# A hybrid decoder trunk on one core: a PSUM bank lent to the recurrences, and values turned by one VectorE transpose with ScalarE copies

## The chip, the cores and the metric

The kernel runs on one core of one Trainium2 chip. The metric is the device time of one execution in microseconds (us). The engines that matter are TensorE (PE in the profile: matmuls; PEld: its weight loads), VectorE (DVE), ScalarE (ACT) and SyncE (SP), which issues the DMAs. PSUM, where matmuls accumulate, is used as eight banks of 128 partitions x 512 f32.

## The reference

One layer of a decoder trunk, for 256 tokens of one new sequence and 8 x 8 tokens of running sequences: 320 columns of tokens, named TOK, in every large matmul. Two token mixers run side by side on one joint projection of x, an mLSTM matrix memory (4 heads) and an HGRN2 linear recurrence (8 heads).

```python
proj = jnp.einsum('btd,de->bte', x, w_in)          # q, k, v, gates of both mixers
h, C, n, m = _mlstm(q, k, v, ig, lf, C0, n0, m0)    # 4 heads, dk 256, dv 512
branch_a = norm(h) * ml_norm_g * sigmoid(ml_o)
o, S = _hgrn2(hq, log f, 1 - f, hg_i, S0)           # 8 heads, dk 128, dv 256
branch_b = rms(o) * hg_norm_g * silu(hg_g)
merged = sigmoid(gate_a) * (branch_a @ w_a) + sigmoid(gate_b) * (branch_b @ w_b)
x1 = LayerNorm(alpha * x + merged @ w_out)
y  = LayerNorm(alpha * x1 + relu(x1 @ w_up)^2 @ w_down)
```

## The kernel before

**Main work.** All projections are cut into 304 tiles of 128 output channels x 320 tokens. A tile has one PSUM bank (a *main* bank, `take` at L545) and 48 matmuls: 16 pieces of the inner dimension, each as three products of split f32 values, `xh` with `wh`, `xl` with `wh` and `xh` with `wl` (high and low halves). A tile's weights come as two *units* of 128x1024, of 24 matmuls each. `prep` (L478) readies a unit: ScalarE rounds the raw weights to the high half (`wh<-wr`), VectorE subtracts to get the low half (`wl<-wr,wh`, L497). There are three buffers for this, so the copy of unit u can start when TensorE has finished unit u−3.

**Side work.** Between the main matmuls stand the small matmuls, copies and transposes of the two recurrences. Each takes a bank from a pool of *side* banks, `sbank`; before the change main has banks 0 to 2 and side banks 3 to 7 (L338, L339). The tiles come in the order of the projection's kinds: q and k of the mLSTM heads, its values (`mv`), then HGRN heads with three kinds of tiles each, with the mLSTM's output gate (`o`) behind them and the HGRN gate (`hg`) behind that.

**What sets the order.** The program is straight-line code, and a scheduler in Python (`Sched`, L144) writes it: each piece of side work is a generator (a chain) that yields an engine, a cost in ns and the instruction. `act` (L261), `dve` (L265) and `dve_t` (L269) give the costs of ScalarE copies, VectorE operations and VectorE transposes. The scheduler adds the costs up to clocks of its own, and issues a chain's next instruction when its clocks say that operands are ready. So the costs decide the order on each engine, and the chip then runs each engine's instructions in that order, with real waits. All ScalarE instructions go through the helper at L350, all plain matmuls through L356.

**The turn.** Values leave their tile as x: channels on partitions, tokens on columns (128 x n x 320, n = 4 blocks for an mLSTM head, 2 for an HGRN head). The recurrences need tokens on partitions. `turn` (L1145) does it in 24 VectorE transposes: for each of 4 groups of 32 partitions, four for the prompt's tokens (L1156, 32 x 64n elements) and two for the others (L1159, 32 x 32n), each of which transposes its 32x32 blocks and puts them on the partitions where they belong. It is called by `m_V` (L948) and by `h_i` (L1474).

**Behind the turn in `h_i`.** ScalarE copies the high half of the turned sample tokens to `rh` (64x256), VectorE subtracts for the low half (L1488, L1492 in the changed kernel), and then two *spread* matmuls `rh,ra` of 128x256 (L356) read `rh`. `h_out` (L1604) computes an HGRN head's outputs, normalises two blocks of 128x256 (`rms`, a ScalarE copy of a bank with an accumulator read), transposes them on VectorE (L1631) and stores them. `ev_o` (L1691) multiplies the mLSTM's normalised output by its gate and splits it to high and low halves for the branch's projection.

Of the kernel before, what the change touches and what calls it, by code (L numbers as in the profile page):

```python
# [20 lines left out]
TOK = 320  # L21
KT = 16
MH, DK, DV = 4, 256, 512
HH, HK, HV = 8, 128, 256
# [220 lines left out]
def wait(*evs):  # L245
    return ("wait", evs)


def acq(pool, n=1):
    return ("acq", pool, n)  # L250


def rel(pool, item):
    return ("rel", pool, item)


def post(ev):
    return ("set", ev)


def act(n, psum=False, ptr=0):  # L261
    return ((61 if psum else 112) + n) / 1.2 + 93 * ptr


def dve(n, psum=False, mode=1, ptr=0):  # L265
    return ((62 if psum else 66) + n / mode) / 0.96 + 55 * ptr


def dve_t(n):  # L269
    return 155.0 + 1.07 * n  # L270


def pe_f(n, m=128):
    return max(212.0 if m == 128 else 162.0, n * 1.66)
# [20 lines left out]
def by_row(ap, off, gap):  # L295

    return cap(ap, off, [[32, 4], [8, 2], [1, 8]] if gap else [[8, 4], [32, 2], [1, 8]])
# [16 lines left out]
class Program:  # L314
# [48 lines left out]
    def carve(self):  # L363
# [12 lines left out]
        self.Part = Part  # L376
        A, B, C, R = Part(self.f1), Part(self.f2), Part(self.f3), Part(self.ra[:, 0:6400])

# [5 lines left out]
        self.vr = Pool([A.three(4, 320)])  # L384
        self.kw = Pool([B.three(2, 320)])
        self.bc = Pool([B(712) for _ in range(2)])
        self.eb0 = B(512)
        self.eb = Pool([self.eb0])
        self.stg = Pool([B(256) for _ in range(2)])
        self.qn0 = B(256)  # L390
        self.qn = Pool([self.qn0])
# [190 lines left out]
    def before(self, i, t):  # L582
        s = self.s
        kind, h, c = t[:3]
        if kind == "mv" and c == 0:
            s.until(lambda: self.vr.free and self.qk.free)
            self.m_start(h)
            self.vr.free.sort(key=lambda x: x[0])
            self.mh[h]["vr"] = self.vr.free.pop(0)[1]
        elif kind == "hf":  # L590
            s.until(lambda: self.hs.free)
            if h == 0:
                s.spawn(self.m_after(), 0)
            self.h_start(h)
        elif kind == "o" and h == 0:
            s.until(lambda: all(m["end"].t is not None for m in self.mh))
        elif kind == "hg" and h == 0:
            s.until(lambda: all(m["end"].t is not None for m in self.hh))
            self.carve_m()
            self.carve_b()  # L600
            B = self.Part(self.f2)
            for pool in (self.sg, self.sg, self.sr, self.ld, self.ld, self.ld):
                pool.free.append((s.t["pe"], B(320)))
        if kind in ("o", "wa", "hg", "wb"):
            s.spawn(self.fetch(kind, h), 1)
        elif kind == "mk" and h == 0 and c == 0:
            self.load_ev.t = s.t["pe"]
            self.dma(self.lmask, self.d["lmask"])
        elif kind == "wo" and h == 0:
            s.until(lambda: len(self.sbank.free) >= 5)  # L610
            self.mbank.free += self.sbank.free[:3]
            del self.sbank.free[:3]
            self.hl_free += [(s.t["pe"], x) for x in self.wx[:4]]
            R = self.Part(self.wxv[4].rearrange("p x s v -> p (x s v)"))
            self.lns = [R.three(2, TOK) for _ in range(3)]
            s.spawn(self.ln_x(), 1)
        elif kind == "dn" and c == 3 and h == 0:
            self.carve_x()
        elif kind == "dn" and c == 0 and h == 0:
            s.spawn(self.xs_(), 0)  # L620
        elif i == len(TILES) - 8:
            for j in range(MH):
                s.spawn(self.m_C(j), 3)
            for j in range(HH):
                s.spawn(self.h_S(j), 3)
# [363 lines left out]
    def m_KW(self, h):  # L989
# [13 lines left out]
        m["khl"] = khl  # L1003
        kh, kl = khl[:, 0], khl[:, 1]
        yield ("dve", dve_t(512), lambda: v.transpose(kw[:, :, 0:256], kw[:, :, 0:256]))
        yield ("act", act(512), lambda: self.A(kh.rearrange("p s k -> p (s k)").rearrange("p (c t) -> p c t", c=2), kw[:, :, 0:256]))
        yield ("dve", dve(512), lambda: v.tensor_tensor(kl, kw[:, :, 0:256], kh.bitcast(F32), ALU.subtract))
# [137 lines left out]
    def turn(self, to, x):  # L1145

        v = self.nc.vector
        n = x.shape[1]
        for a in range(4):
            p = slice(32 * a, 32 * a + 32)  # L1150
            col = lambda y: y.rearrange("p (c a k) -> p a c k", a=4, k=32)[:, a]
            for b in range(4):
                q = slice(32 * b, 32 * b + 32)
                i = x[p, :, 0:NP_].rearrange("p c (i b k) -> p b i c k", b=4, k=32)[:, b]
                o = to[q, 0:2, :].rearrange("p i (c a k) -> p a i c k", a=4, k=32)[:, a]
                yield ("dve", dve_t(64 * n), lambda: v.transpose(o, i))  # L1156
            for b in range(2):
                o, i = col(to[64 + 32 * b:96 + 32 * b, 2, :]), x[p, :, NP_ + 32 * b:NP_ + 32 * b + 32]
                yield ("dve", dve_t(32 * n), lambda: v.transpose(o, i))  # L1159

    def later(self):
        e = Ev()
# [452 lines left out]
    def h_out(self, h):  # L1615
        nc, v, m = self.nc, self.nc.vector, self.hh[h]
        if h:
            yield wait(self.hh[h - 1]["o"])
        yield wait(m["aT"], m["I"])
        at, it = m["at"], m["it"]  # L1620
        on = yield acq(self.on)
        yield post(m["o"])
        b = yield acq(self.sbank)
        yield ("pe", pe_f(256), lambda: self.mm(b[:, 0:256], at[:, 0:128], it[:, 0, :], start=True, stop=True))
        yield ("pe", pe_f(256), lambda: self.mm(b[:, 256:512], at[:, 368:496], it[:, 0, :], start=True, stop=False))
        yield ("pe", pe_f(256), lambda: self.mm(b[:, 256:512], at[:, 128:256], it[:, 1, :], start=False, stop=True))
        for i in range(2):
            yield from self.rms(b[:, 256 * i:256 * i + 256], on[:, i, :], 128)
        yield rel(self.sbank, b)
        for i in range(2):  # L1630
            yield ("dve", dve_t(256), lambda: v.transpose(on[:, i, :], on[:, i, :]))  # L1631
        yield from self.place(self.rows_to(self.oH[h]), on[:, 0:2, :].rearrange("p i v -> p (i v)").rearrange("p (b c) -> p b c", c=32))
        done = self.later()
        yield wait(m["S"])
        ob = m["ob2"]
        yield from self.rms(ob[:, 0:256], on[:, 2, :], 128)
        yield rel(self.sbank, ob)
        yield rel(self.at, at)
        b = yield acq(self.sbank)
        for j in range(2):  # L1640
            yield ("pe", PE_T, lambda: nc.tensor.transpose(b[:, 128 * j:128 * j + 128], on[:, 2, 128 * j:128 * j + 128], self.ident))
        o = yield acq(self.ho)
        for j in range(2):
            yield ("act", act(64, True), lambda: self.A(by_row(o, 64 * j, False), by_row(b, 128 * j, True)))
        yield rel(self.sbank, b)
        yield ("sp", 620, lambda: self.dma(
            self.oL[h].rearrange("(j p) t -> p j t", p=128), o[:, 0:128].rearrange("p (j t) -> p j t", t=64)))
        for j in range(2):
            yield post(self.oT_ev[2 * h + j])
        yield wait(self.later())  # L1650
        yield rel(self.ho, o)
        yield wait(done)
        yield rel(self.on, on)
        yield wait(m["SP"], m["sdone"])
        yield rel(self.it, it)
        yield rel(self.hs, m["set"])
        yield post(m["end"])
# [33 lines left out]
    def ev_o(self, j, c, b):  # L1691
        v = self.nc.vector
        g = yield acq(self.sg)
        r = yield acq(self.sr)
        yield from self.sigmoid(b[:, :TOK], g, r, ((self.mbank, b),))
        yield rel(self.sr, r)
        x = yield from self.fetched("o", j)
        yield ("dve", dve(TOK, ptr=1), lambda: v.scalar_tensor_tensor(g, g, self.vec[:, V_MLG + j:V_MLG + j + 1], x, ALU.mult, ALU.mult))  # L1698
        yield rel(self.ld, x)
        yield from self.split(g, self.bah[:, j, :], self.bal[:, j, :])  # L1700
        yield rel(self.sg, g)
        yield post(self.ba_ev[j])
# [386 lines left out]
```

## Time and profile before

| | us |
|---|---|
| median of 3 runs | 2304.08 |
| lowest, highest | 2303.45, 2305.43 |
| the profiled execution: its time | 2302.73 |
| the profiled execution: its span | 2300.8 |
| busy: PE, DVE, ACT | 2289.6, 1458.9, 1036.6 |

The granted TensorE clock was 0.999 on the mean. The span is the stretch from the first to the last instruction that the profiler recorded. A row of a timeline is: start in us from the span's start, length in us, engine, line, operation, what is written, `<-`, what is read, shapes, count; in brackets the idle time before it and what ended it. A row of groups has the count, then the busy time in us and the mean of one in ns. A row of waits has engine, operand and line, what it waited for, and the total in us, the number of times and the longest. Names: `f`, `f3h` and `f3m` are scratch, `it` and `iv` of the code among them; `bank` is any PSUM bank; `rh` and `ra` are operands of side matmuls.

### The profile page before, as it was taken

The page shows a single profiled execution, that of the slowest core. Times are in us where ns is not written, and L with a number is a line of the kernel's source. Part 1 is how long each engine was busy: PE and PEld are TensorE (multiplying, and loading weights), DVE is VectorE, ACT ScalarE, POOL GpSimd, SP SyncE. Part 2 cuts the span into 40 slices and gives each one's busy share as a digit, 9 for nine tenths or more (in the row PEclk, how much of TensorE's full clock was granted, in tenths as well). Part 3 has the DMA queues.
Part 4 walks back from the last instruction along what each step waited for, and adds up shares of the span by engine and source line. Part 5 has one row for each costly group of instructions (what it writes and reads, how often), then busy time and mean ns, then how long its engine had stood idle before and what let it go on. Part 6 is the DMA issues. An engine that isn't in the chain of part 4 may idle for free.

```text
span 2300.8 us, 38921 instructions
## 1 busy us (share of the span) xinstructions
PE 2289.6 (100%) x15592; PEld 2246.1 (98%) x15592; DVE 1458.9 (63%) x2634; ACT 1036.6 (45%) x1653; POOL 13.5 (1%) x37
## 2 busy tenths in 40 slices
PE   9999999999999999999999999999999999999998
PEld 9999899999999999999999999999999999999998
DVE  6786786788888886555555767654444444444455
ACT  5443445455555565444433446533433343234334
POOL 0000000000000000000000000000000000000000
PEclk9999999999999999999999999999999999999999
DMA  7667977755565564555545644444444444444475
GB/s 284 211 186 259 295 250 229 259 176 185 191 207 187 166 198 167 180 174 170 176 172 175 214 163 147 147 147 149 154 147 150 152 147 153 149 147 154 149 228 193
DMA packets 214574, 424.94 MB, mean 185 GB/s; under 512 B 83572, under 2 KB 110068, under 8 KB 213368
## 3 DMA queue, kind: packets, MB, share of 16 engines
q1 hardware_dynamic: 209512, 415.97, 53.7%
q0 software_dynamic: 4736, 6.29, 1.0%
q8 instruction: 122, 2.00, 0.3%
q14 instruction: 60, 0.49, 0.1%
q10 hardware_dynamic: 144, 0.20, 0.0%
HBM read 371.48 MB, written 50.90 MB: 184 GB/s over the span
## 4 chain that ended last, share of the span: by engine, by line
PE 69%; DVE 3%; ACT 1%; issue 0%; ACTq 0%; DVEq 0%
PE bank L356 69%; DVE wl L497 1%; ACT wh L350 0%; DVE f L1156 0%; DVE f L1445 0%; ACT f L350 0%; DVE f3m L1973 0%; DVE f3m L1980 0%; ACT f3m L350 0%; DVE f L1159 0%; DVE f L1315 0%; DVE f L1316 0%; DVE f L1631 0%; DVE f L1698 0%; DVE f L1309 0%
## 5 line engine op out<-in xcount | busy, mean ns | idle before, releaser
L356 PE MATMUL bank<-xh,wh 128*128 128x320 f32 (+1 forms) x2504 | 794.6, 318 | 0.0
L356 PE MATMUL bank<-xh,wl 128*128 128x320 f32 (+1 forms) x2504 | 774.8, 310 | 0.0
L356 PE MATMUL bank<-xl,wh 128*128 128x320 f32 (+1 forms) x2504 | 772.2, 309 | 0.0
L497 DVE TENSOR_TENSOR wl<-wr,wh 128x1024 fp32r<-128x1024 f32 x440 | 538.7, 1224 | 361.4 <-ACT wh L350 358.3
L350 ACT ACTIVATE wh<-wr 128x1024 fp32r<-128x1024 f32 x440 | 465.4, 1058 | 524.7 <-PE bank L356 495.6
L356 PEld LDWEIGHTS bank<-xh,wh 128*128 128x128 f32 x2504 | 472.0, 189 | 17.2 <-issue 15.3
L356 PEld LDWEIGHTS bank<-xl,wh 128*128 128x128 f32 x2504 | 471.5, 188 | 3.3
L356 PEld LDWEIGHTS bank<-xh,wl 128*128 128x128 f32 x2504 | 471.8, 189 | 0.2 <-DVE wl L497 0.2
L497 DVE TENSOR_TENSOR bb<-wr,bb 128x1024 fp32r<-128x1024 f32 x162 | 198.5, 1225 | 193.7 <-ACT bb L350 193.5
L350 ACT ACTIVATE bb<-wr 128x1024 fp32r<-128x1024 f32 x162 | 171.6, 1059 | 294.6 <-PE bank L356 277.5
L356 PE MATMUL bank<-ra,wh 128*128 128x320 f32 x1008 | 275.9, 309 | 0.7 <-DVE ra L1672 0.7
L356 PE MATMUL bank<-ra,bb 128*128 128x320 f32 x1096 | 255.2, 309 | 0.0
L356 PE MATMUL bank<-xh,bb 128*128 128x320 f32 (+1 forms) x1136 | 253.8, 309 | 0.0
L356 PE MATMUL bank<-rxb,bb 128*128 128x320 f32 x1088 | 249.0, 309 | 0.0
L356 PEld LDWEIGHTS bank<-xh,bb 128*128 128x128 f32 x1136 | 191.0, 188 | 0.0
L356 PE MATMUL bank<-rxb,wh 128*128 128x320 f32 x608 | 187.5, 308 | 0.0
L356 PE MATMUL bank<-rxb,wl 128*128 128x320 f32 x608 | 187.5, 308 | 0.0
L356 PEld LDWEIGHTS bank<-ra,bb 128*128 128x128 f32 x1096 | 184.9, 187 | 0.0
L356 PEld LDWEIGHTS bank<-rxb,bb 128*128 128x128 f32 x1088 | 184.2, 187 | 0.0
L356 PEld LDWEIGHTS bank<-ra,wh 128*128 128x128 f32 x1008 | 180.9, 187 | 0.9 <-DVE ra L1672 0.9
L356 PE MATMUL bank<-xl,bb 128*128 128x320 f32 (+1 forms) x568 | 175.5, 309 | 0.0
L356 PE MATMUL bank<-bb,wh 128*128 128x320 f32 (+1 forms) x536 | 119.0, 313 | 0.0
(259 smaller groups left out, 2244.4 us busy)
## 6 DMA issues: line engine op xcount, KB each, us to landing
wr<-wt SPq DMA_DIRECT2D x602, 512.0 KB, 3.3
rx<-C SPq DMA_DIRECT2D x34, 256.0 KB, 5.6
Cs<-rx SPq DMA_DIRECT2D x34, 256.0 KB, 4.8
f<-C SPq DMA_DIRECT2D x30, 256.0 KB, 5.5
Cs<-f SPq DMA_DIRECT2D x30, 256.0 KB, 4.1
f<-first SPq DMA_DIRECT2D x6, 704.0 KB, 9.6
vD<-ra SPq DMA_DIRECT2D x4, 1024.0 KB, 5.2
f<-S SPq DMA_DIRECT2D x8, 512.0 KB, 5.0
```

What stands on the lines that cost most here:

```text
L350: return self.nc.scalar.activation(out, in_, func, **kw)
L356: self.nc.tensor.matmul(*a, **kw)
L497: self.V().tensor_tensor(lo, raw, hi.bitcast(F32), ALU.subtract)
```

## The change

Five edits:

1. *Banks.* At the first `mk` tile (keys of the first mLSTM head) one main bank is moved to the side pool; at the first `hg` tile, when both recurrences have ended, it is given back. In between main work has two banks and side work six.
2. *The turn.* One VectorE transpose of the whole x in place (128x1280 for an mLSTM head, 128x640 for an HGRN head; L1152) does all 32x32 blocks; the 24 pieces are then copied to their places by ScalarE (`self.A`), each planned as ready when the transpose ends.
3. *The cost of a transpose* in the planner goes from 155 + 1.07n to 295 + 1.05n ns.
4. `h_out` transposes its two blocks in one operation of 128x512 instead of two of 128x256.
5. `ev_o` waits, from block 7 on, until the last HGRN head has reached "aT" or "sdone" before it splits.

```diff
--- before.py
+++ after.py
@@ -267,7 +267,7 @@
 
 
 def dve_t(n):
-    return 155.0 + 1.07 * n
+    return 295.0 + 1.05 * n
 
 
 def pe_f(n, m=128):
@@ -598,12 +598,15 @@
             s.until(lambda: all(m["end"].t is not None for m in self.hh))
             self.carve_m()
             self.carve_b()
+            self.mbank.free.append(self.sbank.free.pop())
             B = self.Part(self.f2)
             for pool in (self.sg, self.sg, self.sr, self.ld, self.ld, self.ld):
                 pool.free.append((s.t["pe"], B(320)))
         if kind in ("o", "wa", "hg", "wb"):
             s.spawn(self.fetch(kind, h), 1)
         elif kind == "mk" and h == 0 and c == 0:
+            s.until(lambda: self.mbank.free)
+            self.sbank.free.append(self.mbank.free.pop())
             self.load_ev.t = s.t["pe"]
             self.dma(self.lmask, self.d["lmask"])
         elif kind == "wo" and h == 0:
@@ -1146,6 +1149,7 @@
 
         v = self.nc.vector
         n = x.shape[1]
+        t = yield ("dve", dve_t(TOK * n), lambda: v.transpose(x, x))
         for a in range(4):
             p = slice(32 * a, 32 * a + 32)
             col = lambda y: y.rearrange("p (c a k) -> p a c k", a=4, k=32)[:, a]
@@ -1153,10 +1157,10 @@
                 q = slice(32 * b, 32 * b + 32)
                 i = x[p, :, 0:NP_].rearrange("p c (i b k) -> p b i c k", b=4, k=32)[:, b]
                 o = to[q, 0:2, :].rearrange("p i (c a k) -> p a i c k", a=4, k=32)[:, a]
-                yield ("dve", dve_t(64 * n), lambda: v.transpose(o, i))
+                yield ("act", act(64 * n), lambda: self.A(o, i), (t,))
             for b in range(2):
                 o, i = col(to[64 + 32 * b:96 + 32 * b, 2, :]), x[p, :, NP_ + 32 * b:NP_ + 32 * b + 32]
-                yield ("dve", dve_t(32 * n), lambda: v.transpose(o, i))
+                yield ("act", act(32 * n), lambda: self.A(o, i), (t,))
 
     def later(self):
         e = Ev()
@@ -1627,8 +1631,7 @@
         for i in range(2):
             yield from self.rms(b[:, 256 * i:256 * i + 256], on[:, i, :], 128)
         yield rel(self.sbank, b)
-        for i in range(2):
-            yield ("dve", dve_t(256), lambda: v.transpose(on[:, i, :], on[:, i, :]))
+        yield ("dve", dve_t(512), lambda: v.transpose(on[:, 0:2, :], on[:, 0:2, :]))
         yield from self.place(self.rows_to(self.oH[h]), on[:, 0:2, :].rearrange("p i v -> p (i v)").rearrange("p (b c) -> p b c", c=32))
         done = self.later()
         yield wait(m["S"])
@@ -1697,6 +1700,8 @@
         x = yield from self.fetched("o", j)
         yield ("dve", dve(TOK, ptr=1), lambda: v.scalar_tensor_tensor(g, g, self.vec[:, V_MLG + j:V_MLG + j + 1], x, ALU.mult, ALU.mult))
         yield rel(self.ld, x)
+        if j > 6:
+            yield wait(self.hh[HH - 1]["aT" if j < 12 else "sdone"])
         yield from self.split(g, self.bah[:, j, :], self.bal[:, j, :])
         yield rel(self.sg, g)
         yield post(self.ba_ev[j])
```

TensorE issues the same number of matmuls. How the rows move is shown for HGRN head 6; in the order rows `f_76` is its turned values (`it`), `f3h` its values before the turn (`iv`), `bank_N` a PSUM bank, `f_75` and `misc` scratch of other chains.

Before, the turn's last pieces on VectorE, between the low halves of two weight units (L497):

```order
L497 TENSOR_TENSOR wl<-wr,wh 128x1024
L1323 TENSOR_SCALAR f_75<-f_75,misc 128x320
L1416 TENSOR_TENSOR f3h<-f3h 128x8x16
L1418 TENSOR_TENSOR f3h<-f3h 128x8x16
L1156 STREAM_TRANSPOSE f_76<-f3h 32x4x32
L1471 COPY_PREDICATED f_75<-lmask,bank_86 128x8x16
L1419 TENSOR_TENSOR f3h<-f3h 128x8
L1156 STREAM_TRANSPOSE f_76<-f3h 32x4x32 x3
L1159 STREAM_TRANSPOSE f_76<-f3h 32x2x32 x2
L497 TENSOR_TENSOR wl<-wr,wh 128x1024
L1416 TENSOR_TENSOR f3h<-f3h 128x4x32
L1488 TENSOR_TENSOR rh<-f_76,rh 64x256
```

The pieces stand between the weight halves, and behind the next L497 comes L1488, which readies `rh`.

Before, ScalarE at the same place, with `rh<-f_76` behind a weight copy and a few operations of other chains:

```order
L350 ACTIVATE wh<-wr 128x1024
L350 ACTIVATE f_76<-bank_85,misc 128x256
L350 ACTIVATE f_75<-f_75,misc 128x320
L350 ACTIVATE f_76<-bank_88 128x4x2x8
L350 ACTIVATE f3h<-f3h 128x128
L350 ACTIVATE f_76<-bank_88 128x4x2x8
L350 ACTIVATE f_75<-bank_83 128x320
L350 ACTIVATE rh<-f_76 64x256
```

After, ScalarE from the weight copies of units 168 and 169 (`x2`; the pieces stand behind the second) up to the copy of unit 170. A form 32x4x32 is a piece for the prompt's tokens, 32x2x32 one for the others:

```order
L350 ACTIVATE wh<-wr 128x1024 x2
L350 ACTIVATE f_76<-f3h 32x4x32 x4
L350 ACTIVATE f_76<-f3h 32x2x32 x2
L350 ACTIVATE f_76<-f3h 32x4x32 x4
L350 ACTIVATE f_76,misc<-bank_84 128x256
L350 ACTIVATE f_76<-f3h 32x2x32 x2
L350 ACTIVATE f_76<-f3h 32x4x32 x4
L350 ACTIVATE f_76<-f3h 32x2x32
L350 ACTIVATE misc<-misc 128x1
L350 ACTIVATE f_76<-f3h 32x2x32
L350 ACTIVATE f_76<-f3h 32x4x32 x2
```

And on from the copy of unit 170 to the copy of unit 171:

```order
L350 ACTIVATE wh<-wr 128x1024
L350 ACTIVATE f_76<-f_76 128x320
L350 ACTIVATE misc<-misc 128x1
L350 ACTIVATE f_76<-f3h 32x4x32 x2
L350 ACTIVATE f_76<-f_76,misc 128x320
L350 ACTIVATE f_76<-f3h 32x2x32 x2
L350 ACTIVATE f_76<-f_76,misc 128x320
L350 ACTIVATE rh<-f_76 64x256
L350 ACTIVATE wh<-wr 128x1024
```

Of the 24 copies 20 stand between the weight copies of 169 and 170 and 4 between those of 170 and 171; `rh<-f_76` stands just ahead of the copy of 171. In heads 2 to 5 they stand in the same way and in head 7 nearly so, twelve units apart.

After, VectorE at the same place, where the L497 shown is that of unit 171:

```order
L1422 TENSOR_TENSOR f3h<-f3h 128x40x4
L497 TENSOR_TENSOR wl<-wr,wh 128x1024
L1319 SCALAR_TENSOR_TENSOR f_76<-f_76 128x320
L1065 TENSOR_TENSOR misc<-misc 128x1
L1423 TENSOR_TENSOR f3h<-f3h 128x40
L1492 TENSOR_TENSOR rh<-f_76,rh 64x256
L1320 SCALAR_TENSOR_TENSOR f_76<-f_76 128x320
```

The 24 transposes are gone from these rows; L1492 stands behind the low half of unit 171.

After, TensorE in unit 170, a quarter of the way through it (`bank_82` is the tile's main bank):

```order
L356 MATMUL bank_81<-f3h 128x64
L356 MATMUL bank_82<-xh,wh 128x320
L356 MATMUL bank_82<-xl,wh 128x320
L356 MATMUL bank_82<-xh,wl 128x320
L1644 MATMUL bank_85<-cst,f_76 128x128
L356 MATMUL bank_86<-rh,ra 128x256
L356 MATMUL bank_82<-xh,wh 128x320
```

The spread matmul `rh,ra` stands behind the first six main matmuls of unit 170; it reads the `rh` that L1492 finishes, which on VectorE stands behind the low half of unit 171. From about the 101st tile on the order on every engine is the same in both kernels, but for the numbers of the banks.

## Prediction

> **What bounds the kernel now.** I read the page first: the span, the busy time of each engine and the span in 40 slices.
>
> ```profile
> span 2300.8 us, 38921 instructions
> PE 2289.6 (100%) x15592; PEld 2246.1 (98%) x15592; DVE 1458.9 (63%) x2634; ACT 1036.6 (45%) x1653; POOL 13.5 (1%) x37
> PE   9999999999999999999999999999999999999998
> DVE  6786786788888886555555767654444444444455
> ```
>
> TensorE is busy from end to end. Work taken from VectorE pays only where TensorE waits for it. So the second view is what TensorE waits for:
>
> ```profile
> PE bank L1530 <- DVE f L987: 1.5, 3, 0.7
> PE bank L356 <- DVE rh L1488: 1.1, 2, 0.6
> PE bank L1212 <- DVE f L1049: 0.7, 1, 0.7
> PE bank L356 <- DVE ra L1672: 0.7, 1, 0.7
> ```
>
> All the waits on VectorE in the whole trace are 4 us, and the last row's lies at 1492 us, far behind the recurrences. The third view is the windows of the HGRN recurrence beside one of the stretch after it:
>
> ```profile
> 500.00:600.00 100.00, 99.95 (x703) 97.28 (x702) 86.16 (x240) 56.01 (x123) 0.73 (x2) 1.00 0.62 197
> 700.00:800.00 100.00, 98.78 (x701) 95.22 (x700) 83.82 (x230) 57.19 (x129) 0.37 (x1) 1.00 0.56 180
> 900.00:1000.00 100.00, 100.00 (x684) 100.00 (x683) 57.77 (x76) 46.78 (x64) 0.00 (x0) 1.00 0.52 177
> ```
>
> VectorE (third busy column) is at 84 to 86% and ScalarE (fourth) at 56%. From the last row TensorE starts a matmul every 100/684 = 0.146 us; a unit of 24 takes 3.51 us, a tile 7.03. Less work on VectorE can give back at most the 4 us of waits. What the 24 pieces per head do on ScalarE, in order between copies that feed TensorE, has no such ceiling.
>
> **The change part by part.**
>
> *Banks.* One of three main banks goes. With two, a tile's bank must be read within the next tile's 7.03 us.
>
> ```profile
> 540.09 0.31 PE L356 MATMUL bank<-xh,wl 128*128 128x320 f32 x1
> ...
> 542.60 0.48 DVE L1309 TENSOR_SCALAR f<-bank 128x320 f32<-128x320 f32 x1
> ```
>
> This is the latest read that I found in the zone: done at 543.08, 3.0 us after the tile's last matmul began. That leaves 4 us: cost nothing. The cover goes if a reader comes 4 us later (a rival below).
>
> *VectorE's turns.* Removed:
>
> ```profile
> L1156 DVE STREAM_TRANSPOSE f<-f 32x128 f32<-32x128 f32 (+1 forms) x160 | 56.9, 356 | 3.8
> L1159 DVE STREAM_TRANSPOSE f<-f 32x64 f32<-32x64 f32 (+1 forms) x80 | 21.2, 265 | 1.9
> L1156 DVE STREAM_TRANSPOSE f<-f3h 32x128 f32<-32x128 f32 x32 | 9.7, 302 | 0.7
> ```
>
> With 16 more pieces of L1159's kind, at most 0.27 each (4 us), that is 92 us of VectorE. Added are 8 operations of 128x640 and 4 of 128x1280, which no trace shows. Two others of that kind bound them:
>
> ```profile
> L1631 DVE STREAM_TRANSPOSE f<-f x16: 424/437/449, 504.1 to 839.1; 128x256 f32<-128x256 f32 x16
> L1090 DVE STREAM_TRANSPOSE f<-f x8: 702/711/712, 117.3 to 392.2; 128x512 f32<-128x512 f32 x8
> ```
>
> The slope is (711−437)/256 = 1.07 ns per element, so 0.85 us and 1.53 us: 12.9 us in all. L1631's 16 operations (7.0 us) become 8 at 0.71 (5.7). VectorE loses 80 us net. All of it lies beside TensorE; its worth is the waits that end in it. Of the waits above, the first three rows lie here: 1.5 + 1.1 + 0.7 = 3.3 us in six. Each is some 0.16 longer than its row says, since a matmul is shown 0.31 long while the next one starts 0.146 behind it: **−4.3 us** at most, and I take that; the other end is 0.
>
> *ScalarE's pieces.* Per HGRN head come 16 copies of 32 partitions x 128 and 8 of 32x64; per mLSTM head 16 of 32x256 and 8 of 32x128. The nearest rows for duration (the last is for a sum below):
>
> ```profile
> L350 ACT ACTIVATE f3h<-f 128x128 f32<-128x128 f32 x12 | 3.7, 306 | 3.8 <-DVE f L1416 3.8
> L350 ACT ACTIVATE f<-f 128x64 f32<-128x64 f32 x8 | 2.0, 247 | 0.0
> L350 ACT ACTIVATE rh<-f 64x256 fp32r<-64x256 f32 x8 | 3.3, 415 | 2.1 <-DVE f L1159 1.9
> L350 ACT ACTIVATE f<-f,misc 128x320 f32<-128x320 f32 x162 | 91.1, 563 | 32.4 <-DVE f L1937 21.3 <-DVE f L1323 7.0
> ```
>
> How close one follows another matters more. Two pictures stand in the timeline:
>
> ```profile
> 740.67 0.24 ACT L350 ACTIVATE f3h<-f3h 128x64 f32<-128x64 f32 x1
> 740.82 0.29 ACT L350 ACTIVATE f<-f3h 128x128 fp32r<-128x128 f32 x1
> 741.02 0.36 ACT L350 ACTIVATE f<-bank 128x256 f32<-128x256 f32 x1
> 741.28 0.19 ACT L350 ACTIVATION_READ_ACCUMULATOR f<-bank 128x1 f32 x1
> ...
> 747.84 1.15 ACT L350 ACTIVATE ra<-bank 32x256 fp32r<-32x256 f32 x3
> ...
> 755.71 0.77 ACT L350 ACTIVATE f<-bank 32x32 f32<-32x32 f32 x4
> ```
>
> Copies over all 128 partitions start 0.10 us before the one ahead ends (0.24 long, next after 0.15). Copies over 32 partitions that step from one group of partitions to another don't: three of 32x256 in 1.15 are 0.383 each, four of 32x32 0.193 each. The pieces step just so. I therefore take 0.32 us for a 32x128 piece and 0.26 for a 32x64 (durations above plus 0.01): 16·0.32+8·0.26 = 7.2 us per head (by the 64x256 row, 9.4 for an mLSTM head). The bounds are 0.20 and 0.15 (overlapped: 4.4 us) and 0.383 and 0.32 (by the 32x256 row: 8.7).
>
> [...]
>
> *Where they stand.* The order rows of head 6 put 20 pieces (14 long, 6 short) between the weight copies of units 169 and 170, and 4 between 170 and 171. The spread matmul `rh,ra` of that head stands a quarter into unit 170 on TensorE; it needs VectorE's L1492, which stands behind VectorE's share (L497) of unit 171, which needs ScalarE's copy of 171. What that chain looks like in time, from before:
>
> ```profile
> 754.31 0.41 ACT L350 ACTIVATE rh<-f 64x256 fp32r<-64x256 f32 x1 [0.56 <-DVE f L1159]
> 754.75 1.06 ACT L350 ACTIVATE wh<-wr 128x1024 fp32r<-128x1024 f32 x1
> ...
> 755.84 1.23 DVE L497 TENSOR_TENSOR wl<-wr,wh 128x1024 fp32r<-128x1024 f32 x1 [1.56 <-ACT wh L350]
> 756.99 0.28 DVE L1416 TENSOR_TENSOR f3h<-f3h 128x128 f32<-128x128 f32 x1
> 757.30 0.42 DVE L1488 TENSOR_TENSOR rh<-f,rh 64x256 fp32r<-64x256 f32 x1
> ...
> 757.12 0.31 PE L356 MATMUL bank<-xh,wl 128*128 128x320 f32 x1
> 757.87 0.35 PE L356 MATMUL bank<-rh,ra 128*128 128x256 f32 x1 [0.43 <-DVE rh L1488]
> ```
>
> L1488 here is L1492 of the change. Put TensorE's start of unit 167 at 0. Three weight buffers let ScalarE's copy 169 start then (+0.1). Until copy 170 it does 1.06 + 14·0.32 + 6·0.26 + 0.55 (a `bank` 128x256 and its accumulator read, as at 741) + 0.2 (a 128x1, as that read) = 7.85: 7.95. Until copy 171: 1.06, two pieces of each size 1.16, three of 128x320 that overlap (0.46 each or less) 1.3, `rh<-f` 0.42, another 128x1 0.2: 4.15, so 12.1. Copy 171 ends at 13.2. Then VectorE: L497 1.15, L1319 with two small ones 0.6 (estimated from L1309's 0.48, as wide), L1492 0.42, and 0.15 to TensorE: **15.5**. TensorE gets there after 3.25 units, 78·0.146 = 11.4, plus side matmuls:
>
> ```profile
> 758.94 0.28 PE L356 MATMUL bank<-rh,ra 128*128 128x256 f32 x1
> 759.06 0.31 PE L356 MATMUL bank<-xh,wh 128*128 128x320 f32 x1
> ...
> 759.36 0.31 PE L356 MATMUL bank<-xh,wl 128*128 128x320 f32 x1
> 759.50 0.38 PE L356 MATMUL bank<-f3h 128*128 128x128 f32 x2
> ...
> 759.87 0.30 PE L356 MATMUL bank<-xl,wh 128*128 128x320 f32 x1
> ```
>
> From 759.36 to 759.87 two main starts and one side matmul pass: 0.51 − 0.29 = 0.22; an `rh,ra` takes 0.12. With some seven of them, 1.3 us: 12.7. The stall is 15.5 − 12.7 = **2.8 us**, and the chain begins anew for each head because ScalarE has idle time between.
>
> *The sum.* In the order, heads 2 to 7 have the same rows at the same place: 6·2.8 = 16.8. Head 1 has fewer pieces between the copies: by the same sum with its rows about 1.7; head 0 about 0.5. The mLSTM heads' pieces have two or more units (7 us) before a matmul reads them; only head 0's spread is tight: 0.5. The merged h_out transpose and the later `split` of ev_o stand where TensorE does not wait for them: 0; the split is needed only by tiles far behind, and if that cover went it would cost its own length, about 1 us. From about 850 us on, all engines' orders are equal, so nothing comes after. Sum: 16.8 + 1.7 + 0.5 + 0.5 − 4.3 = +15.2. Against the profiled execution's own 2302.7 (span 2300.8 and 1.9 around it) that is 2317.9; the runs' median is 1.35 above that execution: 2319.3. I state **2320**.
>
> **The rivals.**
> - *The pieces overlap* as full-width copies do: 0.20 and 0.15, 4.4 us a head, 2.8 less; L1492 comes at 12.7 and the stall is gone, as are the 4.3 us of waits: 2304.1 − 4.3 + 0.5 = 2300.3, not slower. It decides once a long piece is below 0.20. For it: the 128-partition rows. Against: the 32-partition rows. Partial overlap (0.25) gives a stall near 1.4 per head: 2310.
> - *Pieces as slow as 0.383 and 0.32*: 1.25 us more per head, 7 to 8 in all, 2327; with other side matmuls of the recurrence also coming late, 2331. For it: the only 32-partition copies in the trace that cost that much read a bank and are 256 long, so they favour the shorter price.
> - *Two banks are too few*: if an evacuation comes 4 us later than now, TensorE waits at the start of a tile; 0.3 us at each of 100 tiles is +30, above 2335 with the rest. Against: 3.0 of 7.03 us used, and VectorE gets lighter.
> - *Relief worth more than 4 us*: excluded, since TensorE has no more to give.
>
> **How the numbers follow.** Forecast 0.66 (its own range 2311 to 2329: 1.4 to 4.3 us per head); overlap 0.09; partial overlap 0.11; slow pieces 0.11; banks 0.03. The range 2304 to 2333 leaves out most of the overlap case, the banks and a little beyond. A measurement of this kernel can tell about 0.2%, 4.6 us: faster is below 2299.5, slower above 2308.7. Faster gets half of the overlap case, 0.05; same the rest of it and most of the partial one, 0.14; slower 0.81.
>
> **What would show it.** Right: TensorE waits some 3 us once per HGRN head, for `rh` of L1492, every 12 units (42 us and the side matmuls) from head 2 on; 16 copies of 32x128 back to back take over 5 us; VectorE's busy time falls by about 80 us, ScalarE's rises by about 90 (7.2·8 and 9 or so·4); the stretch after 850 us is as before, later by the difference. Wrong: piece starts 0.20 us apart; waits at a tile's first matmul for a bank; waits for `wl` or `wh`, which would mean that the weight copies themselves fell behind.

## The result, and the profile after

The changed kernel takes 2338.66 us (median of 4 runs, 2338.23 to 2339.80) against 2304.67 us for the kernel before (2303.45 to 2305.43): a ratio of 1.0149, with a 95% interval of 1.0131 to 1.0166, or +34 us. The forecast was 2320, its range 2304 to 2333: the direction was right, the size outside the range. The profiled execution took 2339.80 us.

The page of the changed kernel, span and busy time:

```profile
span 2338.0 us, 38951 instructions
PE 2302.4 (98%) x15592; PEld 2258.2 (97%) x15592; DVE 1374.6 (59%) x2350; ACT 1127.6 (48%) x1941; POOL 13.3 (1%) x37
```

VectorE lost 84 us and ScalarE gained 91; the prediction had 80 and 90. TensorE now has idle time, and its waits say for what (operand and line, what it waited for, total us, times, longest):

```profile
PE bank L1644 <- ACT f L350: 17.2, 6, 2.9
PE bank L356 <- DVE rh L1492: 4.1, 2, 2.1
PE bank L356 <- DMA rx<-C: 3.2, 2, 2.1
PE bank L356 <- DVE f L1275: 1.3, 1, 1.3
PE bank L356 <- DVE ra L967: 1.2, 1, 1.2
PE bank L356 <- DVE misc L1059: 1.0, 1, 1.0
```

The first two rows are the eight HGRN heads, 21.3 us; the other four lie in the mLSTM heads, 6.7 us. Of the three rows of before that stood here (3.3 us), the two for `f` are gone; the row for `rh` was at 612 and 758 us, in heads 3 and 6, where the stall of L1644 now stands. Up to 850 us no main matmul is among those that wait. The windows show a second thing (the last three columns are the granted clock, the DMA share and GB/s):

```profile
500.00:600.00 100.00, 97.14 (x673) 94.85 (x671) 66.66 (x163) 62.85 (x156) 0.73 (x2) 0.98 0.59 181
700.00:800.00 100.00, 94.27 (x643) 91.64 (x642) 65.65 (x164) 65.65 (x162) 0.37 (x1) 0.97 0.59 177
900.00:1000.00 100.00, 100.00 (x685) 100.00 (x684) 62.44 (x86) 50.73 (x72) 0.00 (x0) 1.00 0.54 171
```

The granted clock is 0.98 and 0.97 in the recurrence, where before it was 1.00, and 1.00 again behind it. One head at close range, first the windows around its wait:

```profile
655.00:660.00 5.00, 3.41 (x24) 3.15 (x23) 2.88 (x8) 3.82 (x10) 0.00 (x0) 1.00 0.32 105
660.00:665.00 5.00, 3.72 (x17) 3.68 (x18) 4.25 (x13) 2.90 (x8) 0.00 (x0) 0.67 0.70 211
665.00:670.00 5.00, 5.00 (x36) 4.86 (x35) 2.80 (x7) 4.07 (x9) 0.00 (x0) 0.99 0.78 265
```

and then the timeline of the same head on ScalarE, VectorE and TensorE, in order of start:

```profile
645.70 1.06 ACT L350 ACTIVATE wh<-wr 128x1024 fp32r<-128x1024 f32 x1 [2.05 <-PE bank L356]
646.66 3.06 ACT L350 ACTIVATE f<-f 32x128 f32<-32x128 f32 x10
...
653.59 1.06 ACT L350 ACTIVATE wh<-wr 128x1024 fp32r<-128x1024 f32 x1
...
657.49 0.41 ACT L350 ACTIVATE rh<-f 64x256 fp32r<-64x256 f32 x1
657.93 1.06 ACT L350 ACTIVATE wh<-wr 128x1024 fp32r<-128x1024 f32 x1
658.10 0.31 PE L356 MATMUL bank<-xh,wl 128*128 128x320 f32 x1
...
659.02 1.23 DVE L497 TENSOR_TENSOR wl<-wr,wh 128x1024 fp32r<-128x1024 f32 x1 [2.09 <-ACT wh L350]
...
660.57 0.15 DVE L1065 TENSOR_TENSOR misc<-misc 128x1 f32<-128x1 f32 x1
...
660.75 0.47 ACT L350 ACTIVATE f<-bank,misc 128x256 f32<-128x256 f32 x1 [1.76 <-DVE misc L1065]
...
660.86 0.42 DVE L1492 TENSOR_TENSOR rh<-f,rh 64x256 fp32r<-64x256 f32 x1
...
661.28 0.33 PE L1644 MATMUL bank<-cst,f 128*128 128x128 f32 x1 [2.87 <-ACT f L350]
...
661.37 0.36 PE L356 MATMUL bank<-rh,ra 128*128 128x256 f32 x1
...
664.18 0.47 PE L356 MATMUL bank<-xl,wh 128*128 128x320 f32 x1
664.45 0.47 PE L356 MATMUL bank<-xh,wl 128*128 128x320 f32 x1
```

From one weight copy to the next ScalarE takes 7.89 us (the prediction's 7.85) and then 4.34 (4.15). VectorE's L497 follows the late copy at once, L1492 ends at 661.28, and there TensorE goes on, 2.87 us late. The matmul that shows the wait is L1644, just ahead of the spread; what it reads also comes from behind that L497 (L1065, then a ScalarE copy that ends at 661.22), so both operands come within 0.1 us of each other. The last two rows are what the prediction did not see: main matmuls now start 0.27 us apart instead of 0.146. Ahead of the program's end, the trace's clock record has eight stretches of 3.41 us at half the clock, here called clock events: at 184 and 317 us, and one behind each wait of HGRN heads 2 to 7 (552, 607, 662, 716, 771 and 826 us). Each loses up to half of 3.41 us, 1.7.

### The profile page after: what moved, and what is told of

The parts are those of the page before. It is cut to its first block, busy times and chain, and to the rows that moved or that the text cites. A ratio compares the mean times of both kernels' runs of the same rounds, so it can differ in the third digit from the quotient of the medians.

```text
span 2338.0 us, 38951 instructions
## 1 busy us (share of the span) xinstructions
PE 2302.4 (98%) x15592; PEld 2258.2 (97%) x15592; DVE 1374.6 (59%) x2350; ACT 1127.6 (48%) x1941; POOL 13.3 (1%) x37
## 4 chain that ended last, share of the span: by engine, by line
PE 89%; ACT 6%; DVE 2%; DMA 1%; issue 1%; SPq 0%; ACTq 0%; POOL 0%; DVEq 0%; POOLq 0%
PE bank L356 89%; ACT f L350 4%; ACT wh L350 2%; DVE wl L497 1%; DMA rx<-C 1%; DMA Cs<-rx 0%; DMA wr<-wt 0%; DVE f3m L1978 0%; DVE f3m L1985 0%; PE bank L1644 0%; DVE ra L967 0%; ACT f3m L350 0%; DVE f L1319 0%; ACT misc L350 0%; DVE f L1152 0%
## 5 line engine op out<-in xcount | busy, mean ns | idle before, releaser
L497 DVE TENSOR_TENSOR wl<-wr,wh 128x1024 fp32r<-128x1024 f32 x440 | 538.8, 1225 | 454.3 <-ACT wh L350 448.5
L356 PEld LDWEIGHTS bank<-xh,wh 128*128 128x128 f32 x2504 | 476.0, 190 | 17.1 <-issue 15.2
L497 DVE TENSOR_TENSOR bb<-wr,bb 128x1024 fp32r<-128x1024 f32 x162 | 198.5, 1225 | 194.2 <-ACT bb L350 194.0
L350 ACT ACTIVATE f<-f 32x128 f32<-32x128 f32 (+5 forms) x413 | 152.5, 369 | 22.4 <-DVE f L1152 7.5
```

The costliest lines, as they stand in the source:

```text
L350: return self.nc.scalar.activation(out, in_, func, **kw)
L356: self.nc.tensor.matmul(*a, **kw)
L497: self.V().tensor_tensor(lo, raw, hi.bitcast(F32), ALU.subtract)
```

## The experiments

Twelve kernels in four groups. "Before" is the median of the kernel before on the same chip in the same group.

| run | us | before | ratio (95%) |
|---|---|---|---|
| h_vector | 2309.54 | 2303.87 | 1.0022 (1.0013 to 1.0031) |
| m_vector | 2328.13 | 2303.87 | 1.0103 (1.0086 to 1.0120) |
| three_main | 2318.89 | 2303.87 | 1.0061 (1.0046 to 1.0076) |
| bank_only | 2303.44 | 2303.87 | 0.9997 (0.9988 to 1.0007) |
| drop4 | 2317.79 | 2303.74 | 1.0061 (1.0046 to 1.0076) |
| drop8 | 2310.28 | 2303.74 | 1.0027 (1.0016 to 1.0038) |
| true_cost | 2303.12 | 2303.74 | 0.9997 (0.9988 to 1.0007) |
| pairs | 2327.85 | 2303.74 | 1.0103 (1.0088 to 1.0118) |
| true_three | 2300.92 | 2303.60 | 0.9991 (0.9982 to 1.0000) |
| pairs_true | 2303.17 | 2303.60 | 0.9996 (0.9988 to 1.0005) |
| true_roomy | 2296.39 | 2303.60 | 0.9970 (0.9959 to 0.9981) |
| m_drop8 | 2332.89 | 2304.32 | 1.0121 (1.0105 to 1.0138) |

### Which part of the change: h_vector, m_vector, three_main, bank_only

In `h_vector` and `m_vector`, `turn_v` is the old `turn`:

```diff
-        yield from self.turn(it, iv)      # h_vector
+        yield from self.turn_v(it, iv)
-        yield from self.turn(vt, vr)      # m_vector
+        yield from self.turn_v(vt, vr)
```

> The changed kernel, but the eight HGRN heads turn their values as before, in 24 VectorE transposes of the old planned cost; the four mLSTM heads keep the one transpose and the ScalarE pieces. Theory (pieces on ScalarE run 7.3 us per HGRN head where the planner books 4.4, so the weight copy behind them is late, TensorE stalls 3 us and its clock is halved for 3.4 us after): the eight stalls and six of the eight clock events go, about -26 us, 2312 us. Rival (two main banks or the other edits are what costs): stays within 8 us of 2339.

> The changed kernel, but the four mLSTM heads turn their values as before, in 24 VectorE transposes; the HGRN heads keep the ScalarE pieces. Theory: what the trace lost up to 430 us (11 us: waits of 1.4, 2.7, 1.5, 1.1, 1.8 us and two clock events) is due to the mLSTM pieces and goes, 2328 us, while the eight waits of the HGRN heads stay at 2 to 3 us each. Rival (the early loss has to do with banks or the SyncE order): that part stays, 2336 to 2340.

`h_vector` came out at 2309.5 and `m_vector` at 2328.1. In `m_vector` the early waits are gone and those of the HGRN heads have stayed as they were:

```profile
PE bank L1660 <- ACT f L350: 17.2, 6, 2.9
PE bank L356 <- DVE rh L1508: 4.1, 2, 2.1
PE bank L356 <- POOL ones L643: 1.0, 1, 1.0
```

In `h_vector` the HGRN waits are down to two of 0.5 us, the early ones are there, and the clock record is clean but for the end of the program (granted clock 0.999 on the mean, against 0.994 in the changed kernel). So taking out the HGRN pieces gains 29 us, and taking out the mLSTM pieces 10.5. Measured from the kernel before, HGRN pieces without the others cost 24 us and mLSTM pieces 6. The two sums, 40 and 30, lie on both sides of 34: the parts do not simply add, and each of these kernels has an order of its own.

`three_main` takes the lines of the bank move out of the changed kernel, `bank_only` puts them alone into the kernel before:

```diff
+            self.mbank.free.append(self.sbank.free.pop())      # at the first hg tile
...
+            s.until(lambda: self.mbank.free)
+            self.sbank.free.append(self.mbank.free.pop())      # at the first mk tile
```

> The changed kernel without the bank move: three main banks and five side banks throughout. Theory (the pieces): the stalls stay, 2330 to 2342. Rival (two main banks cost, by late evacuation or by what the order makes of them): falls to 2305 or so.

> The kernel before with only the bank move added: two main and six side banks through both recurrences, turns and costs as before. Theory (banks are harmless, evacuation needs 3 of 7 us): within 4 us of the kernel before, 2301 to 2308. Rival (two banks cost): 2315 or more, with TensorE waiting at a tile's first matmul.

`bank_only` gave no difference: two main banks alone cost nothing. `three_main` fell between the two theories, at +15 instead of +34 us. Its waits:

```profile
PE bank L356 <- ACT f3h L350: 5.5, 2, 2.7
PE bank L356 <- DVE rh L1489: 5.0, 3, 2.6
```

With three main banks the same pieces make another order, in which TensorE stalls for more than 0.6 us only four times from 430 us on (up to 474, 650, 756 and 826 us, for 1.9 to 2.7 us), and not once in each of eight heads. Each of the four was met by a clock event, two of them 6.83 us long (granted clock 0.995 on the mean). So the bank move is harmless by itself and more than doubles the loss together with the pieces. Main matmuls don't wait for a bank in either kernel, so what it alters is the order that the planner writes.

### Is it the length of the pieces: drop4, drop8, m_drop8

The order is kept by letting the planner book a piece that is then not issued; the values of those pieces are missing.

```diff
-                yield ("act", act(64 * n), lambda: self.A(o, i), (t,))
+                yield ("act", act(64 * n), lambda: None if n == 2 and b >= 3 else self.A(o, i), (t,))   # drop4
+                yield ("act", act(64 * n), lambda: None if n == 2 and b >= 2 else self.A(o, i), (t,))   # drop8
+                yield ("act", act(64 * n), lambda: None if n == 4 and b >= 2 else self.A(o, i), (t,))   # m_drop8
```

> The changed kernel with the order of every engine kept, but in each HGRN head 4 of the 16 long ScalarE pieces (32x128) are not issued, so those values are not placed. Theory (pieces of 0.317 us in the chain that ends in the spread's rh): the wait of heads 2 to 7 falls from 3.03 to 1.75 us, those of heads 0 and 1 to about 1, that is -10 us; as 1.75 is about the length from which a clock event followed, between none and six of the events of 1.6 us go with it: 2319 to 2329. Rival (the wait has another cause, and the pieces only stand in its shadow): 2339, waits unchanged.

> As drop4, with 8 of the 16 long pieces of each HGRN head not issued. Theory: waits of 0.5 us or less per head, and no clock event from 430 us on, so -19 us of waits and -10 us of clock: 2309 to 2312. If stalls alone counted, without the clock, 2319. Rival (another cause): 2339.

The wait of heads 2 to 7, first in `drop4`, then in `drop8`:

```profile
PE bank L1644 <- ACT f L350: 8.2, 6, 1.4
```

```profile
PE bank L1644 <- ACT f L350: 1.3, 6, 0.2
```

From 2.87 us to 1.37 and 0.22: a piece not issued shortens the wait by 0.3 to 0.4 us until there is little left. In neither profiled execution is there a clock event between 430 us and the end of the program (granted clock 0.999 on the mean in both, 0.994 in the changed kernel). The span fell by 23.5 us from the changed kernel to `drop4` (the medians by 20.9; the profiled execution of `drop4` is the fastest of its four). The waits explain 17.2 − 8.2 = 9.0 in heads 2 to 7 and 4.1 − 0.6 = 3.5 in heads 0 and 1, with 1.4 of DMA wait lost again: 11.1. The remaining 12.4 stand against eight clock events that went, 1.55 us each. The pages bear it out: TensorE's busy time, for the same 15592 matmuls, is 2289.8 us in `drop4` and 2302.4 in the changed kernel, 12.6 more. All eight events went, two more than the expectation allowed for, and `drop4` came out just below its 2319 to 2329. `drop8` at 2310.3 decides against the sum without the clock, 2319.

> The changed kernel with the order of every engine kept, but in each mLSTM head 8 of the 16 long ScalarE pieces (32x256, 0.43 us each) are not issued, so those values are not placed. Theory (the waits at 63, 180, 235, 254 and 314 us are lateness of ScalarE behind the mLSTM pieces, handed on to VectorE and to the state's DMAs): most of these 8 us of waits and the two clock events before 430 us go, 2326 to 2331. Rival (they come from where the order puts state loads and side work): these waits stay, 2336 to 2340. The HGRN waits are the same in both.

It came out at 2332.9, between the two. Waits of the mLSTM part that are left:

```profile
PE bank L356 <- DMA rx<-C: 3.6, 2, 2.6
```

The three waits on VectorE (L967, L1059, L1275) and both early clock events are gone: they were lateness. The waits for the loads of state `C` are not (3.6 us against 3.2; `drop4`, whose mLSTM part is that of the changed kernel, has 4.6). Behind the HGRN stalls the clock events fell otherwise here (granted clock 0.995 on the mean): head 1 has one, that of head 2 is 6.83 us long, and head 4 has none. The expectation had most of all five going; three of five did. `m_vector`, with another order, has none of the two. So the DMA waits seem to come from the order that the pieces make; which step of the order delays those loads was not tried. For one of the three on VectorE, at 316 us in the changed kernel, the path can be read:

```profile
310.12 3.07 ACT L350 ACTIVATE f<-f 32x128 f32<-32x128 f32 x8
313.22 1.06 ACT L350 ACTIVATE wh<-wr 128x1024 fp32r<-128x1024 f32 x1
314.31 1.23 DVE L497 TENSOR_TENSOR wl<-wr,wh 128x1024 fp32r<-128x1024 f32 x1 [2.24 <-ACT wh L350]
315.45 0.74 DVE L1275 SCALAR_TENSOR_TENSOR f<-f,f,bank 128x512 f32<-128x512 f32 x1
316.25 0.50 PE L356 MATMUL bank<-ra 32*128 32x512 f32 x1 [1.26 <-DVE f L1275]
```

The weight copy stands behind eight pieces, L497 waits for the copy, L1275 stands behind L497, and a matmul that reads no piece waits for the bank that L1275 reads.

### Do copies over 32 partitions overlap: pairs

```diff
                 yield ("act", act(64 * n), lambda: self.A(o, i), (t,))
+                if b >= 2:
+                    e = 32 * (b - 2)
+                    o2, i2 = col(to[64 + e:96 + e, 2, :]), x[p, :, NP_ + e:NP_ + e + 32]
+                    yield ("act", act(32 * n), lambda: self.A(o2, i2), (t,))
-            for b in range(2):
...
```

> The changed kernel with the 24 pieces of a head in another order: each of the 8 short pieces stands right behind a long one that reads the same 32 partitions and writes the same 32 partitions. Theory that ScalarE holds a copy back because its group of partitions differs from the last one's: those 8 short pieces start 0.1 us before the long one ends, 0.8 us less per head, waits of 2.2 us for heads 2 to 7, 2333 or less. Rival (copies over 32 partitions never overlap, wherever they lie): starts as far apart as now, 2336 to 2341.

ScalarE at the place that the changed kernel shows as ten pieces in 3.06 us (eight long and two short):

```profile
641.38 2.97 ACT L350 ACTIVATE f<-f 32x128 f32<-32x128 f32 x11
```

Now eleven pieces, eight long and three short, take 2.97. Start to start, a short piece follows a long one on the same 32 partitions (input and output) after 0.216 us, while the long one is 0.309 long. In the changed kernel, where a short piece behind a long one reads the same 32 partitions and writes others, it starts after 0.319; a long one that follows a long one so starts after 0.321 here. So in these two traces the short piece started 0.09 us before the long one ended where both groups were the same, and 0.01 us behind its end (0.307 long there) where the group that it writes differed. The waits of heads 2 to 7 fell from 2.87 to 2.15 us, as expected (2.2):

```profile
PE bank L1645 <- ACT f L350: 12.9, 6, 2.2
```

Only four of these six waits were followed by a clock event (granted clock 0.996 on the mean), and the time was 2327.9.

### Is it the booking: true_cost, true_three, pairs_true, true_roomy

All write the whole output; what changes is the price that the planner has for a piece (in `true_three`, at + 110, also the bank move goes; in `pairs_true` the pieces stand in pairs, at + 115 and + 20).

```diff
-                yield ("act", act(64 * n), lambda: self.A(o, i), (t,))
+                yield ("act", act(64 * n) + 110, lambda: self.A(o, i), (t,))   # true_cost; true_roomy: + 160
-                yield ("act", act(32 * n), lambda: self.A(o, i), (t,))
+                yield ("act", act(32 * n) + 110, lambda: self.A(o, i), (t,))   # true_cost; true_roomy: + 160
```

> The changed kernel with one difference: the planner books each ScalarE piece 110 ns dearer (310 ns for 32x128, 257 for 32x64, 417 for 32x256), which is what they were measured to take one behind another. Nothing is left out. Theory (the pieces are late against the plan, and the order leaves the spread no room): the order now leaves room, waits of HGRN heads under 1 us, no clock events after 430 us: 2305 to 2315. Rival (24 pieces on ScalarE are too much work wherever they stand): over 2325.

> The changed kernel with the pieces booked 110 ns dearer and without the bank move (three main, five side banks). Theory (what cost was the pieces' booked price, and the banks only decided where the lateness hit): about the time of the kernel with the dearer booking and two main banks, 2300 to 2306. Rival (the ScalarE pieces need the sixth side bank to be free of loss): 2310 or more.

> The changed kernel with the pieces in pairs that share their groups of 32 partitions, and booked at what pairs were measured to take (315 ns for a long piece of an HGRN head, 167 for a short one). Theory: the pieces are 0.7 us shorter per head and booked rightly; six waits of 0.6 us at the spread shrink or go: 2299 to 2303, up to 0.2% below the kernel before. Rival (the waits have moved on to another chain): 2303 to 2308.

> The changed kernel with the pieces booked 160 ns dearer, 50 more than measured. Theory (the six waits of 0.6 us for the spread's operand are lateness of ScalarE that the plan does not yet know): they go, 2299 to 2302. Rival (those waits come from the order, not from lateness): 2303 to 2308.

`true_cost` takes all of the 34 us back: 2303.1, no difference from before. Work is the same as in the changed kernel, 24 pieces of the same length on ScalarE; only their places differ. That refutes "too much work for ScalarE wherever it stands". `true_three` is no slower without the bank move (2300.9, interval 0.9982 to 1.0000), so the sixth side bank is not needed. `pairs_true` (2303.2) is no better, its waits have moved to the state's DMAs (4.2 us in three), as its rival had it; its eleven runs spread over 6.6 us, though, from 2299.3 to 2305.9. `true_roomy` is 0.3% faster than the kernel before, 0.2 to 0.4% by the interval, and beats both kernels; 2296.4 is below the expected 2299 to 2302. Its page, and all that TensorE waits for in it:

```profile
span 2294.5 us, 38933 instructions
PE 2286.8 (100%) x15592; PEld 2245.6 (98%) x15592; DVE 1372.3 (60%) x2350; ACT 1127.7 (49%) x1941; POOL 13.4 (1%) x37
```

```profile
PE bank L356 <- POOL ones L643: 1.0, 1, 1.0
PE bank L356 <- DVE ra L1675: 0.7, 1, 0.7
PE bank L356 <- DMA rx<-C: 0.2, 1, 0.2
```

Its timeline shows what the price changed, in the same head as above:

```profile
621.60 2.13 ACT L350 ACTIVATE f<-f 32x128 f32<-32x128 f32 x7
...
624.89 1.06 ACT L350 ACTIVATE wh<-wr 128x1024 fp32r<-128x1024 f32 x1
...
629.34 1.06 ACT L350 ACTIVATE wh<-wr 128x1024 fp32r<-128x1024 f32 x1
630.42 1.47 ACT L350 ACTIVATE f<-f 32x64 f32<-32x64 f32 x5
...
632.85 1.06 ACT L350 ACTIVATE wh<-wr 128x1024 fp32r<-128x1024 f32 x1
...
635.77 0.42 DVE L1492 TENSOR_TENSOR rh<-f,rh 64x256 fp32r<-64x256 f32 x1
...
636.91 0.28 PE L356 MATMUL bank<-rh,ra 128*128 128x256 f32 x1
```

The weight copies now stand 4.5 and 3.5 us apart with pieces between each two, where it was 7.9 us with 20 between two; and `rh` is ready at 636.19, 0.7 us before the spread reads it. The busy times of VectorE and ScalarE are those of the changed kernel within 3 us; none of the HGRN heads has a wait left. `true_cost` had six waits for `rh` there, 3.6 us together.

## Why the prediction was wrong, point by point

Two steps failed: the clock, which the sum did not have, and the mLSTM heads, which it put at 0.5 us.

- **What bounds the kernel**: right, TensorE. The ceiling of 4 us for relief was too low: `true_roomy` gives back 7 us (span −6.3). Waits explain 4.3 of that by the prediction's own reckoning (3.3 us fewer, and 0.16 for each of the six); 2 us come from elsewhere on TensorE, whose busy time is 2.8 us less, and no run isolates them.
- **Banks, cost nothing**: right for the bank move alone (`bank_only`), wrong in company (`three_main`). The step looked at when a bank is read and not at what one more side bank lets the planner do.
- **VectorE's turns**: right. 128x640 took 0.81 us and 128x1280 1.50 (0.85 and 1.53 predicted), 84 us less in all. The waits for `f` went, as taken; the two for `rh` gave place to the stalls of heads 3 and 6, which the sum counts in full.
- **ScalarE's pieces**: right. 32x128 took 0.307 us and 32x64 0.253, with 0.01 between them; full overlap and 0.383 are both excluded.
- **The stall of heads 2 to 7**: right, chain and size: 2.8 predicted, 2.87 by the row of the wait, 3.03 with the 0.16 that the prediction adds to a row. The row names L1644 and not the spread, as L1644 stands ahead of it.
- **Heads 0 and 1**, 0.5 and 1.7: mis-sized. They measured 2.1 and 2.0, 1.9 us more together.
- **mLSTM heads, 0.5**: mis-sized, and the step behind it failed: "The mLSTM heads' pieces have two or more units (7 us) before a matmul reads them; only head 0's spread is tight". That spread waited 1.2 us. The pieces delay the weight copies and with them VectorE's other work, so matmuls that read no piece wait too (the rows at 310 to 316 us show one): 6.7 us of waits in place of 0.5. `m_drop8` removed 3.5 of them; the 3.2 of DMA waits stayed, and their cause is open.
- **The clock**: absent from the sum. A stall was priced at its own length. Behind eight of the stalls TensorE ran 3.41 us at half its clock, 1.55 us each by `drop4`, 12.4 in all. This is the largest term that was missed.
- **The merged transpose of `h_out` and the later `split`, 0**: no run takes them out alone; `true_cost` keeps both and loses nothing.

Added up: the predicted +15.2, 1.9 for heads 0 and 1, 6.2 for the mLSTM waits and 12.4 for the clock are +35.7 us, against 34.0 between the medians and 37.2 between the two spans.

The cause is therefore the planner's price. It booked a piece at 0.20 us that takes 0.32, and so an order was written that leaves the spread no room; the chip paid with a stall in each head, and in six of the eight once more with the clock. No rival had this outcome. The one with two banks came nearest in time (above 2335), and the one with slow pieces had 2331, both for reasons that did not happen: no main matmul waits for a bank, and the pieces took 0.32 and not 0.383. The bank move did count, but through the order (`three_main`).

## What to carry to other kernels

When an operation is moved to another engine under a planner, its price there should be the measured start-to-start time in the pattern it will stand in: here 110 ns on a price turned +34 us into 0 with the same work, and 160 ns turned it into −7. When a stall of TensorE is predicted, its length is not its price: ask whether the clock is cut behind it. Here eight waits of the changed kernel, of 1.26 to 2.87 us, were met by 3.41 us at half the clock, and waits of 2.10 and 1.96 us in heads 0 and 1 were not, as the next section shows. And an edit that is harmless alone can cost together with another, through the order (`bank_only` against `three_main`), so a prediction has to look at the order of both together.

## What the runs showed of the hardware

- In the changed kernel's clock record each of the eight events is 3.413 us long, at half the clock, and any two start a whole number of such lengths apart: from 552.46 to 825.53 us each lies 54.61 us behind the last, 16 times 3.413, and the two early ones, at 183.82 and 316.94 us, are 39 steps of 3.413 apart. With TensorE's waits laid on these steps, the step just ahead of an event holds 1.85 us of waits for the one at 184 us and 2.41 to 2.87 us for the six from 552 us on; for the one at 317 us it holds 1.26 us, and why that event came is open. No other step of this trace holds more than 1.35 us. The waits of 2.10 and 1.96 us of heads 0 and 1, which had no event, lie on two steps each (1.20 and 0.90, 1.35 and 0.60). The kernel before, whose longest wait is 0.71 us once the main matmuls run, has no event ahead of the program's end. The 1.75 us in the expectation of `drop4` is an estimate; it lies between the 1.35 us without an event and the 1.85 us with one, and the event behind 1.26 us speaks against a fixed length. In the other runs, by the length of the wait: in `m_vector` (granted clock 0.995 on the mean) five of six waits of 2.87 us were followed by an event (one event there was two steps long), and of the two of 2.1 and 2.0 us the second had one; of six of 2.15 us four (`pairs`, 0.996), of six of 1.37 us none (`drop4`, 0.999).
- In two patterns of ScalarE's copies over 32 partitions a short piece started 0.216 us behind a long one of 0.309 (`pairs`, both read and write the same 32 partitions) and 0.319 us behind one of 0.307 (the changed kernel, the short one writes others). So 0.09 us of overlap stood against none.
